# A two-block transformer layer on one core: overflow list in three spread steps, and differential attention with both distance products first and one softmax sum moved into the head's RMS norm

## The chip, the cores and the metric

The kernel runs on one core of a Trainium2 chip. The metric is the time of one execution on the device, in microseconds, as the median of several runs. TensorE is the matrix engine, VectorE, ScalarE and GpSimd (POOL) are the other engines, SyncE (SP) issues the weight transfers.

## The reference

Two blocks run one after the other on 512 tokens of 1024 features, all in float32. The first is a hybrid mixer followed by a mixture of experts (64 experts, 8 per token, 256 wide, and one shared expert). The second has two layers: latent attention with a feed-forward network, and then differential attention with a feed-forward network. The change touches the mixture of experts and the differential attention. Cut to those:

```python
def moe(h, w_router, router_bias, w1, w3, w2, ws1, ws3, ws2):
    ...
    counts = jnp.bincount(flat_e, length=N_EXPERTS)
    ...
    def expert_block(args):
        e, toks, gs = args
        xb = t[toks]
        return swiglu(xb, w1[e], w3[e], w2[e]) * gs[:, None]
    ...
    routed = jax.ops.segment_sum(out.reshape(rows, D), row_tok, num_segments=n_tok)

def _diff_mixer(x, w_in, lam_q1, lam_k1, lam_q2, lam_k2, g_sub, w_o, lambda_init):
    ...
    def block(args):                      # 128 queries, 8 heads, two maps m per head
        i, q_b = args
        q_pos = i * Q_BLOCK + jnp.arange(Q_BLOCK)
        dist = jnp.abs(q_pos[:, None] - k_pos[None, :]).astype(f32)
        logits = jnp.einsum('bqhmd,bkhmd->bmhqk', q_b, k, preferred_element_type=f32) * scale
        logits = logits - slopes[:, None, None] * dist
        logits = jnp.where(_chunk_mask(i * Q_BLOCK, s), logits, NEG_BIG)
        p = jax.nn.softmax(logits, axis=-1)
        a = p[:, 0] - lam * p[:, 1]
        o = jnp.einsum('bhqk,bkhe->bqhe', a.astype(v.dtype), v, preferred_element_type=f32)
        return o.astype(x.dtype)
    ...
    o = _rmsnorm(o, g_sub) * (1.0 - lambda_init)
    return o.reshape(b, s, DIFF_HEADS * DIFF_V) @ w_o
```

A head has 64 features per map and 128 for v; the mask lets a query see the keys up to the end of its chunk of 64.

## The kernel before

**Products.** Every float32 product is made of three passes over split operands (a high and a low part): `mm3` issues low x high, high x low and high x high into one PSUM bank (L228, L229, L230). The split itself is ScalarE's copy (L220, names wh, xet, ...) and VectorE's difference (L221, names wl, ...). `trs` transposes on TensorE (L233). PSUM has eight banks, handed out by `ps()`, named b in the trace.

**Weights.** `_Stream` loads weights on SyncE in the order of a job list (L112, name wraw), `raw` jobs ahead, and splits them. Its tiles come from a heap of 22 slots of 128x2048 (`slot`), from which xet, eo, ms and others are taken too; a slot is used again when its last reader is done, so a load can wait on any engine or on a transfer.

**Mixture of experts.** A list of ops is run in a loop; op by op an up product (both halves of an expert's first layer, L228 to L230 on xet) and a down product (L1412 on wraw and aet) follow, in a program order that is written out. Down results are scaled into eo (ScalarE L1414, VectorE L1416) and added to the accumulator in memory by a scattering transfer on POOL (L1217); rows are gathered on POOL (L1212). At op 40 `overflow()` (L1444) makes the list of pairs that did not fit an expert's capacity: counts (L1450, L1451), a chain of small VectorE operations for the capacities (L1454 to L1466), two matmuls (L1468, L1469), a second VectorE chain (L1471 to L1486, names tot, pl, ms), twelve matmuls (L1489) and copies to ll, li, nov (L1492 to L1497). All of it stands in one piece ahead of op 40's down product. The overflow blocks, which read ll, li and nov, come after the last op.

**Differential attention.** `pipeline` runs steps A, B, C, E, F, G, I for each head h and each block of 128 queries qt (nk = 128, 256, 384 or 512 keys), each with its own delay, and between them pieces of the projections of the next head pair as filling. A(h, qt) makes the logits of the two maps in two banks: a product of diag(h) with the distances (L2029), and three passes of q and k, which take rows 0 to 63 of the array for map 0 and rows 64 to 127 for map 1. B takes the maximum (L923, name nm) and the exponential with its sum (ScalarE L926). C combines the maps (L2043 to L2047): p0 is divided by its sum, r1 = -lam/s1, p0 = p1 * r1 + p0. E transposes and splits (pt), F multiplies by v. G squares the output with a sum (L2075), and at qt = 3 makes the norm of the head (`rsqrt`, L240 to L260) and scales into t2k (L2081). I transposes t2k (L233).

The indexer of the first block makes its scores by `mm3` as well, from 64-row operands: two heads that follow each other lie on rows 0 to 63 and 64 to 127 (names kit, qith, qitl).

Of the kernel before, what the change touches and what calls it, by code (L numbers as in the profile page):

```python
# [16 lines left out]
OP = mybir.AluOpType  # L17
# [6 lines left out]
NT = 4  # L24
# [6 lines left out]
NEG = -1e30  # L31
SLOTS = 22
FIX, PAIRS = 2, 16

CAPS = ((2, 128), (5, 192), (16, 128), (24, 96), (32, 80), (50, 64), (64, 48))
LR=9; LA=2; MOE_RAW=7
# [144 lines left out]
class _K:  # L181
# [735 lines left out]
        for _ in fill or ():  # L917
            pass

    def soft_exp(self, ps, nk, name, bufs):  # L920
        nc, V = self.nc, self.nc.vector
        nm = self.sm([128, 1], "nm", bufs=4)
        V.tensor_reduce(nm, ps[:, :nk], AX.X, OP.max, negate=True)  # L923
        p = self.sm([128, 512], name, bufs=bufs)
        sm = self.sm([128, 1], "sum", bufs=6)
        nc.scalar.activation(p[:, :nk], ps[:, :nk], AF.Exp, bias=nm, accum_out=sm)  # L926
        return p, sm

# [157 lines left out]
    def moe_block(self, hT, h2d, x1d):  # L1086
        nc, V, a, st = self.nc, self.nc.vector, self.a, self.st
        st.raw, st.ahead = MOE_RAW, 0
        late = slice(256, 512)
# [13 lines left out]
        acc = self.acc  # L1103
# [102 lines left out]
        def table_upto(n):  # L1206
            while nt[0] < min(n, NB):
                table_step(nt[0])
                nt[0] += 1
# [215 lines left out]
        def transpose_in(u):  # L1425
            if u < len(units):
                for b in range(first[u], first[u + 1]):
                    xT[b] = xpose(xg(b % 4))
# [15 lines left out]
        def overflow():  # L1444

            W = 96
            NB4 = 4
            psq = self.ps()
            for tt in range(NT):
                nc.tensor.matmul(psq[:NE, 0:2], Mp[:, tt], ones[:, 0:2], start=tt == 0, stop=tt == NT - 1)  # L1450
            nc.tensor.matmul(psq[:NE, 2:4], perm_b, evb, start=True, stop=True)  # L1451
            cap = self.sm([NE, 1], "cap", bufs=1)
            f2 = self.sm([NE, 1], "cap2", bufs=1)
            V.memset(cap, float(CAPS[0][1]))  # L1454
            for (e, c0), (_, c1) in zip(CAPS, CAPS[1:]):
                V.tensor_scalar(f2, pid[:NE], float(e), float(c1 - c0), OP.is_ge, OP.mult)
                V.tensor_tensor(out=cap, in0=cap, in1=f2, op=OP.add)
            base = self.sm([NE, NB4], "base", bufs=1)
            for b in range(NB4):
                V.tensor_scalar(base[:, b:b + 1], cap, 128.0 * b, None, OP.add)  # L1460
            cn = self.sm([NE, 4], "cn", bufs=1)
            V.tensor_copy(cn, psq[:NE, 0:4])
            fl = self.sm([NE, NB4], "fl", bufs=1)
            flb = self.sm([NE, NB4], "flb", BF16, bufs=1)
            V.tensor_tensor(out=fl, in0=cn[:, 0:1].to_broadcast([NE, NB4]), in1=base, op=OP.is_gt)
            V.tensor_copy(flb, fl)  # L1466
            psf = self.ps()
            nc.tensor.matmul(psf[:NE, 0:NB4], before[:NE, :NE], flb, start=True, stop=True)  # L1468
            nc.tensor.matmul(psf[:, NB4:2 * NB4], ones[:NE, :], flb, start=True, stop=True)  # L1469
            tot = self.sm([128, NB4 + 1], "tot", bufs=1)  # L1470
            V.memset(tot, 0.0)  # L1471
            for b in range(NB4):
                V.tensor_tensor(out=tot[:, b + 1:b + 2], in0=tot[:, b:b + 1], in1=psf[:, NB4 + b:NB4 + b + 1], op=OP.add)
            pl = self.sm([NE, NB4], "pl", bufs=1)
            V.tensor_tensor(out=pl, in0=tot[:NE, 0:NB4], in1=psf[:NE, 0:NB4], op=OP.add)
            V.scalar_tensor_tensor(pl, fl, -4096.0, pl, op0=OP.mult, op1=OP.add)
            V.tensor_scalar(pl, pl, 4096.0, None, OP.add)
            lst = self.ps()
            tmp = self.slot(F32, "ms")[:NE].bitcast(BF16)
            oh = tmp[:, 0:NB4 * W].rearrange("p (a b) -> p a b", b=W)  # L1480
            col = tmp[:, 1024:1024 + (NB4 + 2) * 128].rearrange("p (a b) -> p a b", b=128)
            V.tensor_copy(col[:, 0], cn[:, 2:3].to_broadcast([NE, 128]))
            V.tensor_copy(col[:, 1], pid[:NE].to_broadcast([NE, 128]))
            for b in range(NB4):
                V.tensor_scalar(oh[:, b], iota_b[:NE, :W], pl[:, b:b + 1], None, OP.is_equal)
                V.tensor_copy(col[:, 2 + b], base[:, b:b + 1].to_broadcast([NE, 128]))  # L1486
            for i in range(3):
                for b in range(NB4):
                    nc.tensor.matmul(lst[:, i * W:i * W + W], col[:, i if i < 2 else 2 + b], oh[:, b],  # L1489
                                     start=b == 0, stop=b == NB4 - 1)  # L1490
            ll = self.const.tile([128, 3, W + 1], F32, name="ll")
            V.memset(ll, 0.0)  # L1492
            V.tensor_copy(ll[:, :, 0:W], lst[:, 0:3 * W].rearrange("p (a b) -> p a b", b=W))
            li = self.const.tile([128, 1], I32, name="li")
            nov = self.const.tile([128, 1], I32, name="nov")
            V.tensor_copy(li, ll[:, 0, 0:1])
            V.tensor_copy(nov, tot[:, NB4:])  # L1497
            self.over = (ll, W), li, nov

        transpose_in(0)  # L1500
        for i, (op, u, m) in enumerate(ops):
            ranks, nb = units[u]
            if i == 2:
                for _ in shared_down():
                    table_upto(min(nt[0] + 1, 9))
            if i == 40:
                overflow()
            if i > len(ops) - 4:
                st.raw = 3
            if i == len(ops) - 8:  # L1510
# [22 lines left out]
            else:  # L1533
# [11 lines left out]
                for b, n in enumerate(nb):  # L1545
                    i = first[u] + b
# [6 lines left out]
        with self.tc.For_i(0, nreg) as _:  # L1553
# [27 lines left out]
            ps = self.ps()  # L1581
# [9 lines left out]
            c, cg = self.sm([128, 8, 3], "tc")[:, :1], self.sm([128, 8, 3], "tg")[:, :1]  # L1591
# [9 lines left out]
            ps = self.ps()  # L1601
# [362 lines left out]
    def diff_block(self, xT, xd, out, early):  # L1964
        nc, V, a, st = self.nc, self.nc.vector, self.a, self.st
# [16 lines left out]
        for i in range(2):  # L1982
            V.tensor_tensor(out=lp[:, i * 64:i * 64 + 64], in0=dc[:, 512 + i * 128:576 + i * 128],
                            in1=dc[:, 576 + i * 128:640 + i * 128], op=OP.mult)
        V.tensor_reduce(lam, lp.rearrange("p (a b) -> p a b", b=64), AX.X, OP.add)
        nc.scalar.activation(lam, lam, AF.Exp)
        nl = self.const.tile([128, 1], F32, name="nlam")
# [5 lines left out]
        def project(hp):  # L1993
# [23 lines left out]
                self.split(vd[:, tt * 256:tt * 256 + 256], vd[:, 1024 + tt * 256:1280 + tt * 256], ps[:, :256])  # L2017
                yield
            cur[hp] = (qd, kd, vd)
        lg, pr, pT, acc = {}, {}, {}, {}  # L2020

        def A(h, qt):
            qd, kd, _ = cur[h // 2]
            nk = (qt + 1) * 128
            o = (h % 2) * 512
            lg[h, qt] = []
            for m in range(2):
                p = self.ps()
                nc.tensor.matmul(p[:, :nk], diag(h), dr[:, 512 - nk:512], start=True, stop=False)  # L2029
                rw = slice(m * 64, m * 64 + 64)  # L2030
                self.mm3(p[:, :nk], (qd[rw, o + qt * 128:o + nk], qd[rw, 1024 + o + qt * 128:1024 + o + nk]),
                         (kd[rw, o:o + nk], kd[rw, 1024 + o:1024 + o + nk]), False, True)
                lg[h, qt].append(p)

        def B(h, qt):
            pr[h, qt] = [self.soft_exp(lg[h, qt][m], (qt + 1) * 128, f"p{m}", 3 - m) for m in range(2)]
            del lg[h, qt]

        def C(h, qt):
            (p0, s0), (p1, s1) = pr[h, qt]  # L2040
            nk = (qt + 1) * 128
            r0, r1 = self.sm([128, 1], "r0", bufs=4), self.sm([128, 1], "r1", bufs=4)
            V.reciprocal(r0, s0)  # L2043
            V.reciprocal(r1, s1)
            V.tensor_tensor(out=r1, in0=r1, in1=nl, op=OP.mult)
            V.tensor_scalar(p0[:, :nk], p0[:, :nk], r0, None, OP.mult)
            V.scalar_tensor_tensor(p0[:, :nk], p1[:, :nk], r1, p0[:, :nk], op0=OP.mult, op1=OP.add)  # L2047

        def E(h, qt):
# [22 lines left out]
        def G(h, qt):  # L2072
            po, ss = acc[h]
            j = self.t2k()
            nc.scalar.activation(j[:, :128], po[:, qt * 128:qt * 128 + 128], AF.Square, accum_out=ss[:, qt:qt + 1])  # L2075
            if qt == NT - 1:
                r = self.rsqrt(ss, NT, 1.0 / 128, 1e-6, "d_r")
                t = self.t2k()
                for i in range(NT):
                    q = slice(i * 128, i * 128 + 128)  # L2080
                    V.scalar_tensor_tensor(t[:, q], po[:, q], r[:, i:i + 1], gsub, op0=OP.mult, op1=OP.mult)  # L2081
                acc[h] = t
# [11 lines left out]
        def fill():  # L2094
            for hp in range(1, 4):
# [3 lines left out]
        st.raw, st.ahead = 2, 1  # L2099
        self.pipeline([(h, qt) for h in range(HEADS) for qt in range(NT)],  # L2100
                      [(A, 0), (B, 1), (C, 2), (E, 3), (F, 4), (G, 5), (I, 6)], fill(), 3,
                      lambda h, qt: h // 2 in cur)
        st.raw, st.ahead = 3, 1
# [52 lines left out]
```

## Time and profile before

| | |
|---|---|
| median of 3 runs | 2502.81 us (2502.02 to 2503.47) |
| profiled execution | 2503.96 us, its span 2502.2 us |
| mean granted clock of TensorE | 0.964 |
| TensorE busy | 2321.1 us, 93% of the span |
| VectorE busy | 1449.6 us, 58% |
| ScalarE busy | 941.1 us, 38% |
| bytes moved | 422.15 MB, mean 169 GB/s |

The profiled execution is one more run, not among the three; 1.76 us of it lie around the span. Rows of the trace give a start in us, a duration, the engine, the line, the operation with output and inputs, a count (several rows of one kind are drawn together), and in brackets the idle time ahead and what ended it. Matmuls overlap in a pipe, so the step from start to start tells what one costs, not its duration.

### The profile page before, as it was taken

How to read it: one execution, taken by the hardware profiler on the slowest of the kernel's cores; microseconds unless marked ns; L12 is line 12 of the kernel's file. 1: busy time of each engine (PE TensorE's matmuls, PEld its weight loads, DVE VectorE, ACT ScalarE, POOL GpSimd, SP SyncE). 2: the span in 40 equal slices, each digit the busy share in tenths (PEclk: the TensorE clock that was granted, in tenths of full speed). 3: DMA queues.
4: the chain of work that ended last, by engine and by line, in shares of the span. 5: the costliest groups of instructions: out<-in, count | busy, mean ns of one | idle time of the engine just before them, and what ended most of it. 6: DMA issues, size and time to landing. Idle time of an engine off the chain costs nothing.

```text
span 2502.2 us, 29499 instructions
## 1 busy us (share of the span) xinstructions
PE 2321.1 (93%) x11088; PEld 1805.0 (72%) x11088; DVE 1449.6 (58%) x2454; ACT 941.1 (38%) x1382; POOL 281.6 (11%) x184
## 2 busy tenths in 40 slices
PE   8877998799989999999699999999999998999998
PEld 4655767567667776676577788888888876888886
DVE  4599666666666765665576653333655657433235
ACT  1552443345545555555244222222234432322121
POOL 0652000122322222231000000000000000000000
PEclk9888999899999999999899999999999998999999
DMA  9442134599998999999402332232231121323310
GB/s 335 169 143 68 51 114 169 175 318 339 331 321 284 378 352 335 369 375 332 125 18 83 103 118 73 96 118 76 83 119 51 51 102 55 114 84 116 102 69 34
DMA packets 195009, 422.15 MB, mean 169 GB/s; under 512 B 21329, under 2 KB 99921, under 8 KB 186545
## 3 DMA queue, kind: packets, MB, share of 16 engines
q1 hardware_dynamic: 169984, 353.44, 39.8%
q0 software_dynamic: 12944, 39.20, 6.7%
q10 hardware_dynamic: 11938, 27.62, 3.0%
q8 instruction: 88, 1.44, 0.2%
q14 instruction: 55, 0.45, 0.1%
HBM read 390.78 MB, written 35.52 MB: 170 GB/s over the span
## 4 chain that ended last, share of the span: by engine, by line
PE 68%; DVE 16%; DMA 9%; ACT 4%; issue 2%; POOL 1%; ACTq 0%; SPq 0%; DVEq 0%; POOLq 0%
PE b L228 20%; PE b L229 19%; PE b L230 19%; PE b L1412 6%; DMA wraw<-in_w_dram 5%; DVE wl L221 4%; PE b L233 4%; DMA acc<-eo,isc 3%; ACT wh L220 2%; DVE work L754 1%; PE b L547 1%; DVE m L750 1%; DMA wraw<-in_w_ada_dram 1%; PE b L2029 1%; DVE y L1651 1%
## 5 line engine op out<-in xcount | busy, mean ns | idle before, releaser
L221 DVE TENSOR_TENSOR wl<-wraw,wh 128x2048 fp32r<-128x2048 f32 (+2 forms) x247 | 557.4, 2260 | 515.5 <-ACT wh L220 465.4
L220 ACT ACTIVATE wh<-wraw 128x2048 fp32r<-128x2048 f32 (+2 forms) x247 | 463.3, 1880 | 152.6 <-DVE wl L221 64.6
L228 PE MATMUL b<-xtl,wh 128*128 128x512 f32 (+1 forms) x928 | 343.5, 370 | 2.9 <-DVE xtl L221 2.9
L229 PE MATMUL b<-xth,wl 128*128 128x512 f32 (+1 forms) x928 | 341.6, 368 | 0.0
L230 PE MATMUL b<-xth,wh 128*128 128x512 f32 (+1 forms) x928 | 341.5, 368 | 0.0
L228 PE MATMUL b<-wl,xet 128*128 128x512 f32 x536 | 231.4, 432 | 15.3 <-DVE wl L221 14.9
L1412 PE MATMUL b<-wraw,aet 128*128 128x512 f32 x536 | 242.0, 595 | 0.8 <-ACT aet L1404 0.8
L230 PE MATMUL b<-wh,xet 128*128 128x512 f32 x536 | 214.2, 400 | 0.0
L229 PE MATMUL b<-wh,xet 128*128 128x512 f32 x536 | 213.1, 398 | 1.1 <-DVE xet L221 0.9
L228 PEld LDWEIGHTS b<-xtl,wh 128*128 128x128 f32 x928 | 176.1, 190 | 32.7 <-DVE xtl L221 3.6
L230 PEld LDWEIGHTS b<-xth,wh 128*128 128x128 f32 x928 | 175.8, 189 | 28.7
L229 PEld LDWEIGHTS b<-xth,wl 128*128 128x128 f32 x928 | 176.0, 190 | 28.0
L1412 PEld LDWEIGHTS b<-wraw,aet 128*128 128x128 f32 x536 | 98.9, 191 | 101.6 <-issue 97.0
L1217 POOL DMA_INDIRECT acc<-eo,isc x67 | 111.4, 1662 | 517.4 <-DMA acc<-eo,isc 126.9
L228 PE MATMUL b<-wl,ath 128*128 128x512 f32 x352 | 137.1, 390 | 0.0
L230 PE MATMUL b<-wh,ath 128*128 128x512 f32 x352 | 136.9, 389 | 0.0
L229 PE MATMUL b<-wh,atl 128*128 128x512 f32 x352 | 136.9, 389 | 0.0
L228 PEld LDWEIGHTS b<-wl,xet 128*128 128x128 f32 x536 | 103.2, 193 | 42.5 <-issue 20.3
L926 ACT ACTIVATE p<-b,nm 128x128 f32<-128x128 f32 (+3 forms) x128 | 67.0, 526 | 166.8 <-DVE nm L923 128.0
L229 PEld LDWEIGHTS b<-wh,xet 128*128 128x128 f32 x536 | 102.8, 192 | 28.6 <-issue 6.5
L230 PEld LDWEIGHTS b<-wh,xet 128*128 128x128 f32 x536 | 102.6, 191 | 23.1
L1933 ACT ACTIVATE t2k<-b 128x512 f32<-128x512 f32 x44 | 26.3, 599 | 185.9 <-PE b L230 185.9
(456 smaller groups left out, 4115.8 us busy)
## 6 DMA issues: line engine op xcount, KB each, us to landing
wraw<-in_w_dram SPq DMA_DIRECT2D x256, 512.0 KB, 11.2
wraw<-in_w_dram SPq DMA_DIRECT2D x64, 1024.0 KB, 9.7
wraw<-in_ffn_w_gu_dram SPq DMA_DIRECT2D x44, 1024.0 KB, 5.1
wraw<-in_w_ada_dram SPq DMA_DIRECT2D x24, 1024.0 KB, 10.4
wraw<-in_ffn_w_down_dram SPq DMA_DIRECT2D x20, 1024.0 KB, 4.9
wraw<-in_diff_w_in_dram SPq DMA_DIRECT2D x12, 1024.0 KB, 5.2
wraw<-in_w_in_dram SPq DMA_DIRECT2D x8, 1024.0 KB, 8.0
wraw<-in_w_in_dram SPq DMA_DIRECT2D x12, 512.0 KB, 5.0
```

The source lines that it names most:

```text
L220: nc.scalar.activation(H, x, AF.Copy)
L221: nc.vector.tensor_tensor(out=L, in0=x, in1=H.bitcast(F32), op=OP.subtract)
L228: mm(ps, s[0], m[1], start=start, stop=False)
L229: mm(ps, s[1], m[0], start=False, stop=False)
L230: mm(ps, s[0], m[0], start=False, stop=stop)
L233: self.nc.tensor.transpose(ps, x, self.ident[:x.shape[0], :x.shape[0]])
L547: nc.tensor.matmul(ps, cb[:, kc, :], w[:, kk, :], start=False, stop=kc == 7)
L750: V.max(m8[qt - 1], work(qt))
L926: nc.scalar.activation(p[:, :nk], ps[:, :nk], AF.Exp, bias=nm, accum_out=sm)
L1217: nc.gpsimd.indirect_dma_start(out=acc, out_offset=IndirectOffsetOnAxis(ap=idx, axis=0), in_=o, in_offset=None, compute_op=OP.add)
L1412: nc.tensor.matmul(ps, aT[:, f * 128:f * 128 + 128], w[:, f, c], start=f == 0, stop=f == 1)
L1933: nc.scalar.activation(sg, pss[j], AF.Silu)
```

## The change

The overflow list becomes a generator of three parts, at ops 40, 41 and 42 of the loop. The first ends after the capacity chain. The second (two matmuls, tot, pl and ms) is run one op later in the loop, the third (twelve matmuls, ll, li, nov) one more. A issues both distance products and then the passes of map 0 and of map 1. The exponentials of map 0 put their sums into one tile s0 of 128x4 per head; C no longer divides p0, and takes r1 = -lam * s0 / s1. The factor s0 that is left in the output is taken out in G: the sums of squares are multiplied twice by r0 = 1/s0 ahead of the norm, and the norm's factor once.

```diff
+OVER = 40
@@
-    def soft_exp(self, ps, nk, name, bufs):
+    def soft_exp(self, ps, nk, name, bufs, sm=None):
@@
-        sm = self.sm([128, 1], "sum", bufs=6)
+        if sm is None:
+            sm = self.sm([128, 1], "sum", bufs=6)
@@ overflow()
             V.tensor_copy(flb, fl)
+            yield
             psf = self.ps()
@@
-            lst = self.ps()
             tmp = self.slot(F32, "ms")[:NE].bitcast(BF16)
@@
+            yield
+            lst = self.ps()
             for i in range(3):
@@
             self.over = (ll, W), li, nov
+            yield
@@
-            if i == 40:
-                overflow()
+            if i == OVER:
+                late = overflow()
+            if i >= OVER:
+                next(late, None)
@@ def A(h, qt)
                 nc.tensor.matmul(p[:, :nk], diag(h), dr[:, 512 - nk:512], start=True, stop=False)
+                lg[h, qt].append(p)
+            for m, p in enumerate(lg[h, qt]):
                 rw = slice(m * 64, m * 64 + 64)
                 self.mm3(...)
-                lg[h, qt].append(p)
@@ def B(h, qt)
-            pr[h, qt] = [self.soft_exp(lg[h, qt][m], (qt + 1) * 128, f"p{m}", 3 - m) for m in range(2)]
+            if qt == 0:
+                s0[h] = self.sm([128, NT], "d_s0")
+            c = s0[h][:, qt:qt + 1]
+            pr[h, qt] = [self.soft_exp(lg[h, qt][m], (qt + 1) * 128, f"p{m}", 3 - m, None if m else c)
+                         for m in range(2)]
@@ def C(h, qt)
-            V.reciprocal(r0, s0)
             V.reciprocal(r1, s1)
-            V.tensor_tensor(out=r1, in0=r1, in1=nl, op=OP.mult)
-            V.tensor_scalar(p0[:, :nk], p0[:, :nk], r0, None, OP.mult)
+            V.scalar_tensor_tensor(r1, r1, nl, t0, op0=OP.mult, op1=OP.mult)
             V.scalar_tensor_tensor(p0[:, :nk], p1[:, :nk], r1, p0[:, :nk], op0=OP.mult, op1=OP.add)
@@ def G(h, qt)
             if qt == NT - 1:
+                r0 = self.sm([128, NT], "d_r0")
+                V.reciprocal(r0, s0.pop(h))
+                for _ in range(2):
+                    V.tensor_tensor(out=ss, in0=ss, in1=r0, op=OP.mult)
                 r = self.rsqrt(ss, NT, 1.0 / 128, 1e-6, "d_r")
+                V.tensor_tensor(out=r, in0=r, in1=r0, op=OP.mult)
```

Two places in TensorE's program show what moves. The first is the overflow list at op 40 (L1450 counts, L1468 and L1469 the two matmuls, L1489 the twelve, L1412 the down product, L1166 the next table step); before, from the last count on:

```order
L1450 MATMUL b<-ones,Mp 64x2
L1451 LDWEIGHTS perm_b
L1451 MATMUL b<-evb,perm_b 64x2
L1468 LDWEIGHTS before
L1468 MATMUL b<-flb,before 64x4
L1469 LDWEIGHTS ones
L1469 MATMUL b<-flb,ones 128x4
L1489 LDWEIGHTS ms
L1489 MATMUL b<-ms 128x96
```

Eleven more pairs on L1489 and then the eight L1412 follow (each is two records in the trace). After the change, from the same place (lines are one to four higher):

```order
L1452 MATMUL b<-ones,Mp 64x2
L1453 LDWEIGHTS perm_b
L1453 MATMUL b<-evb,perm_b 64x2
L1414 MATMUL b<-wraw,aet 128x512 x8
L1471 LDWEIGHTS before
L1471 MATMUL b<-flb,before 64x4
L1472 LDWEIGHTS ones
L1472 MATMUL b<-flb,ones 128x4
L1168 LDWEIGHTS P
L1168 MATMUL b<-idc,P 128x3
```

The down product now stands ahead of the two matmuls, and the twelve (now L1493) come some 40 rows later, between the up and the down product of op 41.

The second place is a group of step A, here the first with 512 keys (L2029 the distance, L228 to L230 the passes of q and k; the two numbers on b are the banks of map 0 and map 1). Before, up to the next transpose:

```order
L2029 MATMUL b_14783<-dr_14412 128x512
L228 MATMUL b_14783<-kd_14432,qd_14431 128x512
L229 MATMUL b_14783<-kd_14432,qd_14431 128x512
L230 MATMUL b_14783<-kd_14432,qd_14431 128x512
L2029 MATMUL b_14788<-dr_14412 128x512
L228 MATMUL b_14788<-kd_14432,qd_14431 128x512
L229 MATMUL b_14788<-kd_14432,qd_14431 128x512
L230 MATMUL b_14788<-kd_14432,qd_14431 128x512
L233 MATMUL b_14811<-ident_71,p0_14700 128x128
```

After:

```order
L2036 MATMUL b_14779<-dr_14412 128x512
L2036 MATMUL b_14781<-dr_14412 128x512
L229 MATMUL b_14779<-kd_14432,qd_14431 128x512
L230 MATMUL b_14779<-kd_14432,qd_14431 128x512
L231 MATMUL b_14779<-kd_14432,qd_14431 128x512
L229 MATMUL b_14781<-kd_14432,qd_14431 128x512
L230 MATMUL b_14781<-kd_14432,qd_14431 128x512
L231 MATMUL b_14781<-kd_14432,qd_14431 128x512
L234 MATMUL b_14803<-ident_71,p0_14701 128x128
```

The two distance products stand together, and the three passes of map 1 follow the three of map 0 directly.

## Rows read from the trace of the kernel before

**Rows 1.** The page, chain that ended last by engine, share of the span.
```profile
PE 68%; DVE 16%; DMA 9%; ACT 4%; issue 2%; POOL 1%; ACTq 0%; SPq 0%; DVEq 0%; POOLq 0%
```

**Rows 2.** Timeline of TensorE around the overflow list: start us, us, instruction, idle before.
```profile
725.37 3.60 PE L1412 MATMUL b<-wraw,aet 128*128 128x512 f32 x8
...
741.57 0.21 PE L1468 MATMUL b<-flb,before 64*64 64x4 bf16 x1 [5.08 <-DVE tot L1471]
...
743.58 1.74 PE L1489 MATMUL b<-ms 64*128 64x96 bf16 x12 [1.68 <-DVE ms L1485]
745.24 8.52 PE L1412 MATMUL b<-wraw,aet 128*128 128x512 f32 x16
```

**Rows 3.** Busy us by stretch: PE, PEld, DVE, ACT, POOL, clock, DMA share, GB/s.
```profile
740.00:760.00 20.00, 16.61 (x68) 10.21 (x69) 9.88 (x39) 3.56 (x4) 3.01 (x2) 0.83 0.51 155
...
2010.00:2020.00 10.00, 10.00 (x67) 8.03 (x65) 5.01 (x18) 3.99 (x13) 0.00 (x0) 1.00 0.00 1
...
2030.00:2040.00 10.00, 7.23 (x22) 5.35 (x23) 8.84 (x30) 2.76 (x11) 0.00 (x0) 0.66 0.40 155
```

**Rows 4.** Timeline of VectorE in the overflow list.
```profile
738.55 0.14 DVE L1456 TENSOR_SCALAR cap<-pid 64x1 f32<-64x1 f32 x1
...
741.93 0.16 DVE L1473 TENSOR_TENSOR tot<-tot,b 128x1 f32<-128x1 f32 x1 [0.41 <-PE b L1469]
...
744.31 0.21 DVE L1486 CAST ms<-base 64x128 bf16<-64x128 f32 x1
```

**Rows 5.** Waits of SyncE's queue, 600 to 900: us in total, times, longest.
```profile
SPq L112 <- DMA acc<-eo,isc: 39.4, 4, 23.1
```

**Rows 6.** Timeline of POOL: the second scatter after the overflow list.
```profile
758.46 1.44 POOL L1217 DMA_INDIRECT acc<-eo,isc  x1 [5.55 <-DMA acc<-eo,isc]
```

**Rows 7.** Timeline of TensorE: one group of step A with 512 keys.
```profile
2017.13 0.39 PE L2029 MATMUL b<-dr 128*128 128x512 f32 x1
2017.45 0.50 PE L228 MATMUL b<-kd,qd 64*128 64x512 f32 x1
2017.78 0.39 PE L229 MATMUL b<-kd,qd 64*128 64x512 f32 x1
2018.02 0.39 PE L230 MATMUL b<-kd,qd 64*128 64x512 f32 x1
2018.34 0.49 PE L2029 MATMUL b<-dr 128*128 128x512 f32 x1
2018.76 0.49 PE L228 MATMUL b<-kd,qd 64*128 64x512 f32 x1
...
2019.65 0.33 PE L233 MATMUL b<-ident,p 128*128 128x128 f32 x1
```

**Rows 8.** Timeline of TensorE: scores of the indexer, two heads at a time.
```profile
121.33 0.50 PE L228 MATMUL b<-kit,qith 64*128 64x512 f32 x2
121.66 0.40 PE L229 MATMUL b<-kit,qitl 64*128 64x512 f32 x2
121.90 0.40 PE L230 MATMUL b<-kit,qith 64*128 64x512 f32 x2
...
122.92 0.50 PE L228 MATMUL b<-wl,hth 128*128 128x512 f32 x1
```

**Rows 9.** Groups of VectorE, 1851 to 2096, by form: busy us, mean ns, idle before.
```profile
L2045 DVE TENSOR_TENSOR r<-r,nlam 128x1 f32<-128x1 f32 x32 | 5.1, 160 | 1.1
...
L2046 DVE TENSOR_SCALAR p<-p,r 128x512 f32<-128x512 f32 x8 | 3.8, 480 | 0.0
```

**Rows 10.** Timeline of VectorE: start of the unbroken stretch after 1907.
```profile
1907.88 2.29 DVE L221 TENSOR_TENSOR wl<-wraw,wh 128x2048 fp32r<-128x2048 f32 x1 [1.38 <-ACT wh L220]
```

**Rows 11.** Timeline of TensorE: two of its waits in the differential attention.
```profile
1915.89 0.66 PE L233 MATMUL b<-ident,t2k 128*128 128x128 f32 x4 [0.19 <-DVE t2k L2081]
...
2032.77 0.79 PE L228 MATMUL b<-wl,mixoh 128*128 128x512 f32 x1 [3.85 <-ACT p L926]
```

**Rows 12.** Waits of TensorE, 1851 to 2096: us in total, times, longest.
```profile
PE b L233 <- DVE t2k L2081: 4.6, 4, 2.9
```

More of the change, by code (lines that the diff above doesn't have):

```diff
@@ L2019, in project @@
             cur[hp] = (qd, kd, vd)
-        lg, pr, pT, acc = {}, {}, {}, {}
+        lg, pr, pT, acc, s0 = {}, {}, {}, {}, {}
         def A(h, qt):
@@ L2032, in A @@
                          (kd[rw, o:o + nk], kd[rw, 1024 + o:1024 + o + nk]), False, True)
-                lg[h, qt].append(p)
         def B(h, qt):
-            pr[h, qt] = [self.soft_exp(lg[h, qt][m], (qt + 1) * 128, f"p{m}", 3 - m) for m in range(2)]
+            if qt == 0:
[3 more added lines that the diff above has]
+                         for m in range(2)]
             del lg[h, qt]
         def C(h, qt):
-            (p0, s0), (p1, s1) = pr[h, qt]
+            (p0, t0), (p1, s1) = pr[h, qt]
             nk = (qt + 1) * 128
-            r0, r1 = self.sm([128, 1], "r0", bufs=4), self.sm([128, 1], "r1", bufs=4)
-            V.reciprocal(r0, s0)
+            r1 = self.sm([128, 1], "r1", bufs=4)
             V.reciprocal(r1, s1)
-            V.tensor_tensor(out=r1, in0=r1, in1=nl, op=OP.mult)
-            V.tensor_scalar(p0[:, :nk], p0[:, :nk], r0, None, OP.mult)
+            V.scalar_tensor_tensor(r1, r1, nl, t0, op0=OP.mult, op1=OP.mult)
             V.scalar_tensor_tensor(p0[:, :nk], p1[:, :nk], r1, p0[:, :nk], op0=OP.mult, op1=OP.add)
```

## The prediction

> **What bounds the kernel now.** I read the chain of waits first, then three stretches: the overflow list in the MoE, the distance and logit products of the differential attention, and an earlier stage of the same kernel that already holds the pattern which the change makes. TensorE carries 68% of the chain [rows 1], so a gain has to be an idle gap of TensorE that closes, or TensorE time that goes while its neighbours keep up.
>
> In the overflow list both exist. TensorE idles 5.08 us before L1468, which waits for the capacity chain on VectorE, and 1.68 us before L1489, which waits for ms; 12 small products then take 1.74 us, and the sixteen L1412 records after them need 8.52 us [rows 2]. In that 20 us window TensorE is busy 16.61 us, its granted clock is 0.83, and the DMA share is 0.51 [rows 3]. In the differential attention (1851 to 2096) TensorE has no idle in most windows, as at 2010 [rows 3], with VectorE busy half the time; what counts there is how long each group on L2029 and L228 to L230 is.
>
> **Overflow list, part by part.** Part 1 stays where it was, but TensorE now goes on to the sixteen L1412 records. The capacity chain runs on VectorE from 738.55 until L1468 starts at 741.57 [rows 2, 4]. L1412 would start where the gap began, 741.57 - 5.08 = 736.5. Ten microseconds earlier eight such records took 3.60 with the clock at its full 2.4 GHz [rows 2], some 0.43 each, so sixteen last 6.9 us; the 8.52 of now comes from the half clock, 1.2 GHz, after the two gaps, which the window's 0.83 holds. It ends near 743.4, after the chain, so the two matmuls of part 2 wait for nothing. Before, L1412 ended at 745.24 + 8.52 = 753.8 [rows 2]. That is 753.8 - 743.4 = 10.4 us earlier. Back go the two matmuls of part 2, in line with other short ones (0.35), and the 12 of part 3 at full clock (12 x 0.1 = 1.2, at most the 1.74 of now). Part 3's inputs come from VectorE work that lasts from 741.9 to 744.5 before [rows 4] and now stands behind the same down product: some 3 us, and a whole up product of TensorE lies between, so I take its wait at zero. The sum is **10.4 - 1.6 = 8.8 us**.
>
> Behind part 3's wait stands op 41's down product, and nobody else waits; ll, li and nov are read only by the overflow blocks after the last op. The order on SyncE and POOL doesn't change. Which slot a weight load takes does, because ms is made later: the load that now waits 23.1 us for a scatter [rows 5] takes a slot last read by matmuls before that down product. I estimate SyncE idle for 10 us instead of 23. The transfers come back sooner than TensorE gains, so they don't eat the 8.8. But the slot of the scattered tile goes to a wh, so that ScalarE's split now stands behind the second scatter, which was issued at 758.46 [rows 6] and will be issued some 8 us earlier. My estimate is 0 to 4 us on ScalarE, of which about 1 reaches TensorE, since the split is made some microseconds ahead of its use. I put the MoE at **-8** (8.8 - 0.8), between -5 (a full 4 us wait) and -10.
>
> **Logit products.** A group with 512 keys is, before the change: distance, three passes of map 0, distance, three passes of map 1. Its starts run from 2017.13 to 2019.65, 2.52 us, eight matmuls [rows 7]. Two passes of one kind follow each other at 2018.02 - 2017.78 = 0.24; the steps between a 128-row and a 64-row matmul are 0.32, 0.33, 0.32 and 0.42. The change puts both distance products first, so one of the two round trips goes, and sets map 0's passes (rows 0 to 63) next to map 1's (rows 64 to 127). What two such sets cost side by side is shown by the indexer's scores on L228 to L230, where two heads lie on the same halves of the rows and come in the same program order, three passes of one and then three of the other: the records start in pairs ("x2"), 121.33, 121.66, 121.90, so twelve matmuls of 512 columns last 122.92 - 121.33 = 1.59 us instead of 12 x 0.23 = 2.8 [rows 8]. A pair costs what one costs.
>
> So the new group is 0.23 (distance) + 0.32 + three pairs (0.33 + 0.24 + 0.33) = 1.45, and saves 1.07: three passes of 0.23 (0.69) and one round trip (0.38). For 384, 256 and 128 keys I scale the passes with the columns and keep the 0.38: 0.90, 0.73, 0.55. One head has all four, 3.25 us; eight heads give **26 us** of TensorE time. The bounds: without pairing 0.1 to 0.38 per group is left (3 to 12 us); below nothing it can't go, since the same eight matmuls run with fewer switches.
>
> **VectorE.** Per group it loses one reciprocal, one product of 128x1 (0.16) and one scaling of p (0.48 at 512) [rows 9]. In eight heads G gains a reciprocal and three products of 128x4, about 0.2 each with the wait on the one before: +0.8. Where VectorE already ends last, part of the 26 is lost. From 1907.88 [rows 10] to 1916 it runs without a break, from the weight split over two maxima to the norm of a head and the t2k scaling, and TensorE waits 0.19 for t2k [rows 11]; the two groups in that stretch (256 and 128 keys, 1.3 us) are lost there, and the chain is 0.8 - 0.4 longer: 1.7 us. The same pattern comes once more, 60 us on (1.7). At 2032.77 TensorE waits 3.85 for ScalarE's exp behind four transfers and a split; part of a group ahead of that is lost (0.6) [rows 11]. The waits for t2k come to 4.6 us in four places [rows 12], most of it in the last head; there I lose 1.2. In the other heads the timeline shows VectorE idle ahead of G's work, more than the few tenths that a head gains. Sum: 26 - 3.4 - 0.6 - 1.2 = 20.8, and for a clock drop after one of the new gaps I take off 0.3: **-20.5**.
>
> Both parts: -28.5. The profiled execution took 2503.96 us (span 2502.2, and 1.76 around it) and would take 2475.5; it lies 1.15 above the median of the runs, 2502.81, so the median becomes **2474**.
>
> **The rivals.**
> 1. *Pairs only where they touch.* TensorE keeps program order, so that only the last pass of map 0 runs beside the first of map 1. Each group then saves one pass and the round trip: 0.62, 0.56, 0.50, 0.45, some 17 us, less 5 lost: -12, and with the MoE -20: 2483. For: nothing but the order of the program. The Trainium skill, "TensorE: Matmul & The Clock Gate" (Part 3, The mechanism), says that matmuls start and end in strict program order, which would make this the outcome; the scores disagree, with same-line records starting in pairs though the program lists them three passes apart [rows 8]. Chance 8%.
> 2. *No pairing.* The scores' pairs could come from something that this group lacks (here the accumulation starts with a full-height matmul). Then 3 to 12 us of TensorE less some 3 of waits, with the MoE: -8 to -17, about 2490. Chance 7%.
> 3. *VectorE or the weight stream takes more.* If a third of the heads are held by VectorE instead of two and the last, or the wh slot keeps TensorE waiting 4 us, 7 to 9 us are lost: 2482. VectorE's 5.01 of 10 us [rows 3] is room on the average, not at the pinches. Chance 8%.
> 4. *Slower: waits that drop the clock.* With shorter groups VectorE could end last in all eight heads, the whole 20.5 be lost to gaps, and each gap be followed by some 5 us at 1.2 GHz instead of 2.4, as after 2032.77, where the window's clock is 0.66 [rows 3]: 8 x 2.5 = 20 more. Total -8 + 20 = +12: 2515. It decides from four such drops on, with the gain all lost. Against it: the two pinches of now have gaps of 0.2 only [rows 11]. Chance 3%, with another 2% for ending within 0.2%.
> 5. *The overflow list brings nothing*, because transfers hold TensorE anyway: -20, 2482. Against it: both gaps are ended by VectorE, not by a transfer [rows 2]. Chance 2%.
>
> **The numbers.** The forecast, 2474 with its own bounds 2465 to 2482 (MoE -5 to -10, the pinches 3 to 8 us, pairs as the scores' [rows 8] or a little better), has 70%. The range that holds it 8 times in 10 reaches to rivals 1, 3 and 5 and the near part of 2: 2465 to 2488. About 0.2% (5 us) is what a measurement can tell from no change. Faster: the forecast, 1, 2, 3 and 5 together, 0.95; the same 0.02; slower 0.03.
>
> **What would show it.** Right: the 5.08 and 1.68 gaps gone, no L1414 record at half clock, SyncE's longest wait for a scatter under 15 us; logit passes L229 to L231 on kd as x2 rows with starts 0.24 apart and a 512 group of 1.4 to 1.5 us; the stage from 1851 to 2096 some 20 us shorter, with two new gaps of 1 to 2 us before a transpose of t2k. Wrong: single rows on kd (rival 1 or 2), a wait of wh for a scatter with TensorE idle behind it, a granted clock of half in many windows of that stage.

## The result, and the profile after

The changed kernel takes 2478.28 us (median of 4 runs, 2476.24 to 2479.69) against 2502.41 of the kernel before (4 runs): ratio 0.9899, 95% interval 0.9885 to 0.9914, so 24.1 us less where 28.5 were forecast. The profiled execution of after took 2478.60 us, its span is 2476.8, the granted clock 0.963.

The chain of the page is still TensorE's; the share of DMA in it fell from 9% [rows 1] to 6%.

```profile
PE 69%; DVE 17%; DMA 6%; ACT 5%; issue 2%; POOL 1%; ACTq 0%; SPq 0%; DVEq 0%; POOLq 0%
```

**Overflow list.** Timeline of TensorE, after; it answers to [rows 2]:

```profile
733.74 7.13 PE L1414 MATMUL b<-wraw,aet 128*128 128x512 f32 x16
740.81 0.19 PE L1471 MATMUL b<-flb,before 64*64 64x4 bf16 x1
740.93 0.17 PE L1472 MATMUL b<-flb,ones 64*128 64x4 bf16 x1
...
748.07 0.68 PE L1493 MATMUL b<-ms 64*128 64x96 bf16 x12
...
766.80 0.77 PE L229 MATMUL b<-wl,xet 128*128 128x512 f32 x1 [3.87 <-DVE wl L222]
```

Both gaps are gone: the down product runs at full clock (7.13 us with its last record's end, before 8.52), and neither the two small matmuls nor the twelve on ms (L1493) wait for anything. But 26 us behind the two small ones there is a new gap of 3.87 us. ScalarE's timeline shows whose it is:

```profile
755.70 0.38 ACT L1406 ACTIVATE aet<-b 128x256 f32<-128x256 f32 x1 [2.59 <-PE b L234]
762.42 1.91 ACT L221 ACTIVATE wh<-wraw 128x2048 fp32r<-128x2048 f32 x1 [6.33 <-DMA acc<-eo,isc]
```

A split stood 6.33 us behind the second scatter. The stretches of TensorE show the price: the window that had 16.61 us busy [rows 3] is full now, and the next one, full before, has 16.13 with a clock of 0.83. The second window before, and then both after:

```profile
760.00:780.00 20.00, 20.00 (x98) 14.08 (x97) 14.19 (x17) 12.07 (x14) 6.14 (x4) 1.00 0.90 256
```

```profile
740.00:760.00 20.00, 20.00 (x111) 14.51 (x110) 13.83 (x35) 7.11 (x9) 5.39 (x3) 1.00 1.00 336
760.00:780.00 20.00, 16.13 (x62) 10.55 (x61) 11.78 (x13) 10.88 (x12) 6.57 (x4) 0.83 0.90 260
```

Both programs have the same 11088 matmul records in nearly the same order, so they can be lined up one by one. Across the overflow list (records 2940 to 3110) TensorE gains 9.05 us; in the 150 records behind it loses 6.96 again. SyncE's longest wait for a scatter, 600 to 900, fell from 23.1 [rows 5] to 8.0 us:

```profile
SPq L113 <- DMA acc<-eo,isc: 15.3, 3, 8.0
```

**Differential attention.** A group with 512 keys, timeline of TensorE, after; it answers to [rows 7]:

```profile
1996.67 0.63 PE L2036 MATMUL b<-dr 128*128 128x512 f32 x2
1997.23 0.51 PE L229 MATMUL b<-kd,qd 64*128 64x512 f32 x2
1997.57 0.40 PE L230 MATMUL b<-kd,qd 64*128 64x512 f32 x2
1997.81 0.39 PE L231 MATMUL b<-kd,qd 64*128 64x512 f32 x2
1998.13 0.33 PE L234 MATMUL b<-ident,p 128*128 128x128 f32 x1
```

The passes come in pairs, and the group lasts 1998.13 - 1996.67 = 1.46 us instead of 2.52. The groups with 384, 256 and 128 keys last 1.17, 0.88 and 0.75 (before 2.07, 1.62 and 1.37), and all 32 groups together 34.3 us instead of 60.9. The whole stage, from its first product to the next network (records 7920 to 9600), before and then after; the first number behind the length is TensorE's busy time, the clock is third from the end:

```profile
1842.16:2155.32 313.16, 295.11 (x1683) 244.13 (x1681) 191.59 (x488) 112.84 (x288) 0.00 (x0) 0.96 0.21 71
```

```profile
1834.58:2129.99 295.41, 270.59 (x1682) 231.54 (x1681) 188.96 (x458) 111.20 (x290) 0.00 (x0) 0.95 0.23 75
```

The stage is 17.75 us shorter. TensorE is busy 24.5 us less, but idles 24.8 instead of 18.05. The granted clock summed over the stage gives 27.3 us at the half clock (1.2 GHz) before and 30.7 after, so, if TensorE was busy in these stretches, 1.7 us of the busy time after is the slower clock, and the work itself shrank by 26.2, close to the 26.6 of the groups. The waits of TensorE, 1840 to 2080, answer to [rows 12]:

```profile
PE b L234 <- DVE t2k L2097: 9.7, 4, 3.5
PE b L229 <- ACT p L928: 4.5, 1, 4.5
```

Of the 25.4 us between the two profiled executions 5.2 have no part of the change in them: 3.1 us lie in the first 240 records and 2.1 around 1445 us, ahead of the first feed-forward network, where the kernel before had run longer at the half clock; the change touches neither place.

### The profile page after: what moved, and what is told of

Its sections match the earlier page's. It is cut to its first block, busy times and chain, and to the rows that moved or that the text cites. A ratio compares the mean times of both kernels' runs of the same rounds, so it can differ in the third digit from the quotient of the medians.

```text
span 2476.8 us, 29476 instructions
## 1 busy us (share of the span) xinstructions
PE 2293.9 (93%) x11088; PEld 1791.6 (72%) x11088; DVE 1445.9 (58%) x2422; ACT 938.8 (38%) x1382; POOL 280.3 (11%) x184
## 4 chain that ended last, share of the span: by engine, by line
PE 69%; DVE 17%; DMA 6%; ACT 5%; issue 2%; POOL 1%; ACTq 0%; SPq 0%; DVEq 0%; POOLq 0%
PE b L229 20%; PE b L230 19%; PE b L231 19%; PE b L1414 7%; DMA acc<-eo,isc 4%; PE b L234 4%; DVE wl L222 4%; ACT wh L221 2%; DVE work L755 1%; PE b L548 1%; DVE m L751 1%; DMA wraw<-in_w_ada_dram 1%; DVE y L1658 1%; DVE nm L924 1%; DVE y L1657 1%
## 5 line engine op out<-in xcount | busy, mean ns | idle before, releaser
L230 PE MATMUL b<-xth,wl 128*128 128x512 f32 (+1 forms) x928 | 341.2, 368 | 0.0
L230 PE MATMUL b<-wh,xet 128*128 128x512 f32 x536 | 214.3, 400 | 0.9 <-DVE xet L222 0.8
L230 PEld LDWEIGHTS b<-xth,wl 128*128 128x128 f32 x928 | 175.5, 189 | 28.2
L230 PE MATMUL b<-wh,atl 128*128 128x512 f32 x352 | 136.9, 389 | 0.0
L230 PEld LDWEIGHTS b<-wh,xet 128*128 128x128 f32 x536 | 104.0, 194 | 28.0 <-issue 6.2
```

The source lines that it names most:

```text
L230: mm(ps, s[1], m[0], start=False, stop=False)
```

## The experiments

All runs are compared with the kernel before on the same chip; runs 1 to 4, 5 to 8 and 9 to 12 were on three different ones. A kernel's runs spread over 3 to 16 us there, so the times decide only what is far apart. The rest is decided by the gaps in the profiles, above all the two pinches: the two places in the middle of the differential attention where TensorE waits for t2k, whose gaps repeat to some hundredths from profile to profile.

**1. The overflow list alone.** Kernel before with this edit:

```diff
-            if i == 40:
-                overflow()
+            if i == OVER:
+                late = overflow()
+            if i >= OVER:
+                next(late, None)
```

and the three `yield`s of the change.

> Kernel before with the overflow list in three steps alone; attention as before. Theory 1 (the two gaps close, and the split that now takes the slot of the scattered tile waits for the second scatter and gives most of it back): TensorE 9 us earlier after the overflow list, 6 to 7 us lost again behind the scatter, in all 1 to 4 us faster than before. Theory 2 (the forecast: the wait hardly reaches TensorE): 7 to 9 us faster.

Measured: 2497.27 us against 2501.82, ratio 0.9973 (0.9961 to 0.9984). TensorE gained the same 9.05 us across the list and lost 2.2 behind the scatter, where ScalarE's split waited 3.8 us; the profiled run was the fastest of the ten, 2493.0. Timeline of TensorE:

```profile
763.51 0.47 PE L229 MATMUL b<-wl,xet 128*128 128x512 f32 x1 [1.35 <-DVE wl L222]
```

The mechanism is theory 1's, the time lies between the two: how much is lost again differs with the split's wait, which was 6.33 us in the changed kernel's profile and 3.82 here.

**2. Step A alone.** Kernel before with the two lines of A moved:

```diff
+                lg[h, qt].append(p)
+            for m, p in enumerate(lg[h, qt]):
                 rw = slice(m * 64, m * 64 + 64)
...
-                lg[h, qt].append(p)
```

> Kernel before with the new order in step A alone; softmax sums and overflow list as before. Theory 1 (pairs of passes give the whole gain, and the sum put into the norm lengthens VectorE's chain where VectorE ends last): groups of 1.45 us at 512 keys, 18 to 22 us faster than before, so at least as much as the differential attention of the changed kernel gained (17.8). Theory 2 (the shorter C is needed so that VectorE keeps up): 10 to 15 us faster.

Measured: 2481.61 us against 2501.82, ratio 0.9914 (0.9891 to 0.9937). The stage is 19.3 us shorter than before, 1.6 more than with the whole change. The two pinches, timeline of TensorE:

```profile
1905.54 0.66 PE L233 MATMUL b<-ident,t2k 128*128 128x128 f32 x4 [1.55 <-DVE t2k L2082]
...
1961.17 1.11 PE L233 MATMUL b<-ident,t2k 128*128 128x128 f32 x4 [1.55 <-DVE t2k L2082]
```

So the pairs give the gain, and the relief in C isn't needed for it: theory 1.

**3. The sum in the norm alone.** Kernel before with the edits of B, C and G.

> Kernel before with the first map's sum put into the norm alone; order of step A and overflow list as before. Theory 1 (TensorE bounds the stage outside the pinches, the pinches get 0.4 us longer): 0 to 2 us slower than before, nothing that the runs can tell. Theory 2 (VectorE's work in C counts): 2 to 5 us faster.

Measured: 2506.5 us against 2501.82, ratio 1.0016 (1.0003 to 1.0029): 4.7 us slower, more than theory 1 allowed. Both pinches grew from 0.19 [rows 11] and 0.20 to 1.02:

```profile
1913.78 0.66 PE L233 MATMUL b<-ident,t2k 128*128 128x128 f32 x4 [1.02 <-DVE t2k L2090]
...
1973.94 0.80 PE L233 MATMUL b<-ident,t2k 128*128 128x128 f32 x4 [1.02 <-DVE t2k L2090]
```

In this profile the stage is 6.1 us longer: 2.3 more idle, and 37.5 instead of 27.3 us at the half clock, which costs half the difference, 5.1, less 1.3 of shorter work. Of these 10.2 us, 3.4 lie behind the second pinch, the rest in and behind the last head. Theory 1 had the sign and the pinches, but in this profile the clock that fell cost more than the gaps.

**4. The three steps at op 41.** Changed kernel with another number:

```diff
-OVER = 40
+OVER = 41
```

> Changed kernel with the three steps at ops 41, 42 and 43, so that the slot of the scattered tile goes to a weight load on SyncE and no longer to a split on ScalarE. Theory 1 (the split's wait for the scatter costs 6 to 7 us): ScalarE waits for no scatter near 760, and the time is 4 to 7 us below the changed kernel, 2471 to 2475. Theory 2 (TensorE has run ahead of the weight transfers and loses it in any arrangement): same time as the changed kernel, 2478.

Measured: 2477.72 us against 2501.82, ratio 0.9893 (0.9872 to 0.9913), the changed kernel's within the interval, as theory 2 said. ScalarE waits no more near 760, but at 783.15 for the scatter of the next tile, whose slot also goes to a split:

```profile
783.15 1.91 ACT L221 ACTIVATE wh<-wraw 128x2048 fp32r<-128x2048 f32 x1 [3.85 <-DMA acc<-eo,isc]
```

TensorE stood 1.38 us behind it and lost 1.9 there. The wait was moved, not removed. Theory 2 has the time, theory 1 the place: the loss goes where the split's wait goes. That the smaller loss doesn't show in the time is in part the clock: the profiled run, the slowest of the four (2482.62), had 37.5 us at the half clock in the differential attention, the changed kernel's 30.7.

**5. Overflow list and step A, without the sum.** The first two edits together.

> Changed kernel without the move of the first map's sum into the norm (overflow list in three steps and the new order in step A). Theory 1 (the sum in the norm only lengthens the two pinches and the tail): the two gaps before the transposes of t2k are 1.55 us instead of 2.37, and the time is 1 to 4 us below the changed kernel, 2475 to 2477. Theory 2 (the relief in C is worth it): 2 to 5 us above it.

Measured: 2476.99 us against 2502.12, ratio 0.9891 (0.9868 to 0.9915). The gaps are 1.53, without the overflow list 1.55. Theory 1 holds in the gap; the 1.3 us below the changed kernel's first median can't be told by time. Why the sum costs 0.83 a pinch and not 0.4 is seen in VectorE's timeline of the stretch. This run first:

```profile
1896.51 0.15 DVE L2050 RECIPROCAL r<-sum 128x1 f32<-128x1 f32 x1
...
1896.83 0.41 DVE L2053 TENSOR_SCALAR p<-p,r 128x384 f32<-128x384 f32 x1
1897.28 0.62 DVE L2054 SCALAR_TENSOR_TENSOR p<-p,r,p 128x384 f32<-128x384 f32 x1
1897.81 0.42 DVE L222 TENSOR_TENSOR pt<-b,pt 128x256 fp32r<-128x256 f32 x1
1898.15 0.16 DVE L241 TENSOR_SCALAR rs_t<-d_ss 128x4 f32<-128x4 f32 x1
```

and the changed kernel:

```profile
1897.16 0.15 DVE L2056 RECIPROCAL r<-sum 128x1 f32<-128x1 f32 x1
1897.35 0.22 DVE L2057 SCALAR_TENSOR_TENSOR r<-r,nlam,d_s 128x1 f32<-128x1 f32 x1
1897.60 0.62 DVE L2058 SCALAR_TENSOR_TENSOR p<-p,r,p 128x384 f32<-128x384 f32 x1
1898.43 0.42 DVE L222 TENSOR_TENSOR pt<-b,pt 128x256 fp32r<-128x256 f32 x1 [0.21 <-ACT pt L221]
1898.78 0.17 DVE L2089 RECIPROCAL d_r<-d_s 128x4 f32<-128x4 f32 x1
1899.05 0.36 DVE L2091 TENSOR_TENSOR d_ss<-d_ss,d_r 128x4 f32<-128x4 f32 x2
1899.44 0.17 DVE L241 TENSOR_SCALAR rs_t<-d_ss 128x4 f32<-128x4 f32 x1
...
1901.23 0.16 DVE L2093 TENSOR_TENSOR d_r<-d_r,d_r 128x4 f32<-128x4 f32 x1
```

C is shorter: its last operation starts 0.44 us behind its first, in run 5 0.77. But VectorE then waits 0.21 for ScalarE's half of the split of pt, which comes behind two exponentials, and the split starts 1.27 us behind C's first operation, in run 5 1.30: C's relief is gone at once. The additions in G stay whole: 1899.44 - 1898.78 = 0.66 ahead of the norm and 0.2 behind it.

**6. Step I one step later.** Changed kernel with

```diff
-                      [(A, 0), (B, 1), (C, 2), (E, 3), (F, 4), (G, 5), (I, 6)], fill(), 3,
+                      [(A, 0), (B, 1), (C, 2), (E, 3), (F, 4), (G, 5), (I, 7)], fill(), 3,
```

> Changed kernel with step I (the transposes of t2k) one step later in the pipeline. Theory 1 (TensorE loses at the pinches because it reaches the transposes before VectorE has made t2k, and the half clock comes from these gaps): both gaps of 2.37 us and the half clock behind them go, nothing is lost elsewhere, 4 to 8 us below the changed kernel, 2470 to 2474. Theory 2 (VectorE bounds the stage there, so that the next wait takes the gap over): the gaps come back before the transposes of p, same time.

Measured: 2479.44 us against 2502.12, ratio 0.9908 (0.9886 to 0.9931). Theory 1 fell (first pinch, timeline of TensorE):

```profile
1903.56 0.50 PE L229 MATMUL b<-xtl,wh 128*128 128x512 f32 x1 [2.36 <-DVE t2k L2097]
```

Both gaps keep their size to 0.02 us and stand before a filling product now, so theory 2 was right that another wait takes them over, but not which. That product writes b and doesn't read t2k: what it can wait for is its PSUM bank, the head's output, which VectorE's t2k reads last. So t2k has to end early, whoever reads it.

**7. Overflow list and step A, with step I later.**

> The kernel of the run with overflow list and step A alone, with step I one step later. Theory 1: with the pinches gone the sum in the norm matters in the tail only, so this is within 1 us of the run with step I later, 2470 to 2474. Theory 2 (C's relief counts once the pinches are gone): 2 to 4 us above that run.

Measured: 2472.42 us (4 runs, 2467.21 to 2473.66) against 2502.12, ratio 0.9873 (0.9849 to 0.9897). That is 7.0 below run 6, which neither theory has. The gaps are 1.53, as in run 5, so step I isn't what made it faster. The stage had 27.3 us at the half clock in this profile, in run 5 it had 34.1; run 10 is the same kernel again.

**8. As run 6, with the reload on SyncE.** The four transfers of y in the out projection's first half move from ScalarE's queue:

```diff
-            X.append(self.reload(xd))
+            X.append(self.reload(xd, nc.sync))
```

with `reload` issuing on the engine it is given.

> Changed kernel with step I one step later and the four reloads of the residual (y from xd) issued by SyncE instead of ScalarE. Theory 1 (the 4.48 us gap before the out projection's first half is ScalarE's: 2.45 us of issuing ahead of the split): that gap is 2 to 2.5 us, and the time is 2 to 4 us below the run with step I later. Theory 2 (the gap is the weight's arrival): no change of the gap.

Measured: 2479.48 us against 2502.12, ratio 0.9905 (0.9884 to 0.9927). Timeline of TensorE:

```profile
2011.63 0.50 PE L229 MATMUL b<-wl,mixoh 128*128 128x512 f32 x1 [1.88 <-ACT p L928]
...
2016.72 0.55 PE L234 MATMUL b<-ident,p 128*128 128x128 f32 x3 [1.28 <-DVE t2k L2097]
```

The gap fell from 4.49 in run 6 to 1.88, by 2.6 where theory 1 had 2.45, and a part came back as a wait for t2k, 1.28. The time didn't follow: the stage had 37.5 us at the half clock in this profile, in run 6 30.7. A gain of 1 us isn't to be shown with these runs.

**9. The slot to a load.** The kernel of run 7, with one more weight load ahead for six ops, which shifts the heap by a tile so that no split takes the scattered tiles' slots there:

```diff
+            if 42 <= i <= 48:
+                st.raw = 10 if i < 48 else LR
```

> The kernel of the run with overflow list, step A and step I later, with one more weight load ahead (10 instead of 9) during ops 42 to 47, so that the slot of the scattered tile goes to a load on SyncE. Theory 1 (the split's wait for the scatter makes the loss near 766): no wait of ScalarE's split for a scatter between 750 and 775, no gap of TensorE there, TensorE keeps the 9 us to within 1, and the time is 2 to 4 us below the run with overflow list, step A and step I later. Theory 2 (weight transfers are late there in any arrangement): the gap stays, now behind a load.

Measured: 2472.88 us (4 runs, 2471.29 to 2474.39) against 2501.44, ratio 0.9883 (0.9861 to 0.9906). No split of ScalarE waits for a scatter between 735 and 800. The loss window of the changed kernel is full:

```profile
760.00:780.00 20.00, 20.00 (x98) 14.06 (x97) 14.41 (x17) 12.08 (x14) 6.08 (x5) 1.00 0.95 302
```

TensorE keeps its 9.05 us to 0.02. SyncE's queue waits for scatters now (waits of SyncE, 735 to 800):

```profile
SPq L113 <- DMA acc<-eo,isc: 21.2, 4, 8.8
```

and that costs TensorE nothing here. Theory 1, but the time is further below run 10 than its 2 to 4 us; run 10 shows why.

**10. Run 7's kernel again,** beside run 9.

> The same kernel as the run with overflow list, step A and step I one step later (no sum in the norm), once more beside the others. If its 2472.4 came from step I: 4 to 6 us below the changed kernel again. If it came from chance in the half clock and in the scatter: 1 to 3 us below it.

Measured: 2479.54 us (5 runs, 2477.70 to 2481.90) against 2501.44, ratio 0.9910 (0.9891 to 0.9930): 1.9 us below the changed kernel beside it, 7.1 above its own median of before. So 2472.42 was not step I's. On one chip run 9 is 6.7 us below run 10, and their programs differ only in the one more load ahead that moves the slot. The profiled executions, 6.6 apart, show that the loss at the slot's place is a part of it. There run 10 loses 4.3 us and run 9 nothing. Another 5.9 lie near 950, where ScalarE's split stands behind a later scatter, as it did in the kernel before. The kernel before, then run 10 and run 9 with ScalarE's row and TensorE's:

```profile
950.70 1.91 ACT L220 ACTIVATE wh<-wraw 128x2048 fp32r<-128x2048 f32 x1 [8.63 <-DMA acc<-eo,isc]
```

```profile
947.23 1.91 ACT L221 ACTIVATE wh<-wraw 128x2048 fp32r<-128x2048 f32 x1 [9.89 <-DMA acc<-eo,isc]
951.61 0.77 PE L229 MATMUL b<-wl,xet 128*128 128x512 f32 x1 [5.20 <-DVE wl L222]
```

```profile
940.48 1.91 ACT L221 ACTIVATE wh<-wraw 128x2048 fp32r<-128x2048 f32 x1 [5.22 <-DMA acc<-eo,isc]
944.86 0.47 PE L229 MATMUL b<-wl,xet 128*128 128x512 f32 x1 [0.54 <-DVE wl L222]
```

Run 7, the same kernel as run 10 on another chip, had the short wait too, 5.20 with a gap of 0.51, and its profiled execution was 5.9 us below run 10's. So the short wait near 950 can come without the slot, and that the slot brought it in run 9 is not shown. In the differential attention run 9 was 2.9 us longer than run 10, with 37.5 us at the half clock and not 30.7. The slot is shown to be worth the 4.3 us at its own place.

**11. The changed kernel again.**

> The changed kernel once more, beside the others: 2476 to 2480. TensorE's gap behind the scatter is ScalarE's wait less 2.45 us again, whatever the wait is this time; the two gaps before the transposes of t2k are 2.37 us again.

Measured: 2481.44 us (6 runs, 2473.95 to 2483.68) against 2501.44, ratio 0.9914 (0.9895 to 0.9934). Its median is 1.4 us above the expected range. ScalarE's wait and TensorE's gap, one fence from each engine's timeline:

```profile
763.91 1.91 ACT L221 ACTIVATE wh<-wraw 128x2048 fp32r<-128x2048 f32 x1 [6.03 <-DMA acc<-eo,isc]
```

```profile
768.29 0.77 PE L229 MATMUL b<-wl,xet 128*128 128x512 f32 x1 [3.56 <-DVE wl L222]
```

6.03 - 3.56 = 2.47. The first profile gave 6.33 - 3.87 = 2.46, run 4's other tile 3.85 - 1.38 = 2.47. The pinches were 2.36 each.

**12. The passes in turn.** Changed kernel with the order of the six passes changed:

```diff
-            for m, p in enumerate(lg[h, qt]):
-                rw = slice(m * 64, m * 64 + 64)
-                self.mm3(...)
+            for x, y in ((0, 1024), (1024, 0), (0, 0)):
+                for m, p in enumerate(lg[h, qt]):
+                    rw = slice(m * 64, m * 64 + 64)
+                    nc.tensor.matmul(p[:, :nk], qd[rw, x + o + qt * 128:x + o + nk],
+                                     kd[rw, y + o:y + o + nk], start=False, stop=not (x or y))
```

> Changed kernel with the passes of the two maps issued in turn (first of map 0, first of map 1, second of map 0, and so on). Theory 1 (TensorE pairs matmuls of different row groups whatever their order within a few instructions): groups as in the changed kernel, 1.45 us at 512 keys. Theory 2 (strict order, so that neighbours pair best): groups shorter by 0.1 to 0.3 us.

Measured: one run, 2483.8 us. The group (all six passes are on one line now):

```profile
1886.84 0.63 PE L2036 MATMUL b<-dr 128*128 128x512 f32 x2
1887.40 0.97 PE L2041 MATMUL b<-kd,qd 64*128 64x512 f32 x6
1888.30 0.33 PE L234 MATMUL b<-ident,p 128*128 128x128 f32 x1
```

1888.30 - 1886.84 = 1.46, as with three and three: theory 1.

## Why the prediction was right, and where it was off

The time lay in the range, 4 us above the forecast. By its own steps:

- **"10.4 - 1.6 = 8.8 us"** for the overflow list: right. Lined up record by record, the nine later profiles with the steps at op 40 gained 9.05 us each, too.
- **"0 to 4 us on ScalarE, of which about 1 reaches TensorE"**: this step failed. The wait was 3.0 to 6.3 us in the nine profiles with this slot, TensorE's gap is that less 2.46, and half of the time at 1.2 GHz behind the larger gaps comes on top: 1.35 to 6.96 us given back, the most in the first profile (gap and clock account for it to within 0.9 us). I had found the slot and the queue, but took the landing of the second scatter from an issue 8 us earlier. It was issued only 6.1 us earlier (752.39 for 758.46) and took 9.9 us to land (762.27), where in the kernel before it had taken 4.8, so it landed only 1.0 us earlier. The DMA share of that window is 1.00, before 0.51 [rows 3]; that the load on the transfers made the scatter slower is likely, but not shown. Run 9 is the test of the slot: with it given to a load, the loss is gone.
- **"eight heads give 26 us"** of the logit products: right, 26.6 by the groups. The pairs are what they were in the scores [rows 8]. Rival 1 is out by the paired rows of the changed kernel and by run 12, whose order would have made the group shorter if only neighbours paired, and left it at 1.46 us. The Trainium skill, "TensorE: Matmul & The Clock Gate" (Part 3, The mechanism), has matmuls start and end in strict program order; the traces disagree, 1.46 us in both orders.
- **"the chain is 0.8 - 0.4 longer"** at the pinches: the 0.8 was right, but hardly any of the 0.4 was to be had, since C's relief ended in a wait for ScalarE (run 5). With 1.53 of gap from the shorter groups and 0.83 from the sum, each pinch is 2.37 instead of 0.19. TensorE's idle time in the stage rose by 6.8 us, where the forecast gave 5.2.
- **"for a clock drop after one of the new gaps I take off 0.3"**: 1.7 in the first profile, 3.4 in run 11. Of the two gaps of 2.37 us one was followed by the half clock, the other not:

```profile
1900.00:1910.00 10.00, 7.63 (x33) 5.86 (x31) 6.81 (x25) 2.96 (x12) 0.00 (x0) 0.83 0.00 1
...
1950.00:1960.00 10.00, 7.63 (x46) 6.28 (x45) 9.11 (x29) 2.81 (x11) 0.00 (x0) 1.00 0.22 86
```

So the stage comes to 26.2 - 6.8 - 1.7 = 17.7 us, forecast 20.5, and the MoE to 9.05 - 6.96 + 0.7 (the drift up to its end) = 2.8, forecast 8. Their sum is 20.5, where 28.5 were forecast and the medians show 24.1. In the profiled pair the rest is the 5.2 us in places that the change doesn't touch, and on the chip of run 11 the changed kernel was 20.0 us below the kernel before. So a part of how near the first time came to 2474 is luck; how the 3.6 us of the medians divide stays open.

The rivals: slower by clock drops (4) had the right mechanism for run 3, which was slower by 4.7 us, but the 26 us of the pairs are far above it. Rival 3 is the nearest to what happened, and its 2482 fits run 11's 2481.44 better than the forecast does. Of its two mishaps one came, the split's wait, at up to 7 us; the other came in another form: VectorE held TensorE in the forecast's places, two heads and the last, but at 2.2 us per pinch and not 1.7.

The version that the experiments point to, run 9, leaves the sum out of the norm and gives the slot to a load: 2472.88 us, ratio 0.9883, 8.6 us below the changed kernel on the same chip; a part of that is the shorter wait near 950, which isn't shown to come from the slot.

## What to carry to other kernels

Two sets of 64-row matmuls that stand next to each other on the two halves of the rows cost here what one set costs (six passes of 512 columns 0.90 us, three of them before 0.89 [rows 7]), so it pays to bring them together, and a stage of the same kernel that has them already gives the price beforehand. Where tiles come from one heap, a moved allocation changes who waits for whom: look up which engine takes the slot of every tile that a slow transfer reads, and see that it is a load ahead of need, not a split on whose result the next product waits. The place near 950, where the kernel before already had such a split, shows that it is worth looking for more than one. Work taken off VectorE was worth almost nothing at the pinch, because its next input wasn't there yet (0.21 us of waiting in run 5's comparison); work added where it ended last was paid in full (0.83 us a pinch).

## What was not expected of the hardware

TensorE's gap behind the split was the split's wait less 2.46 us in every profile with that wait, to 0.02, and near 950 the wait less 4.68 in all fourteen, to 0.01. The clock wasn't so regular: a gap of 1.02 us (run 3, at 1973.94) was followed by the half clock and one of 2.37 (1958.91, after) was not, and two kernels with the same gaps in this stage to 0.3 us, runs 7 and 9, had 27.3 and 37.5 us at the half clock, a difference of 5 us in time. The same kernel in two comparisons on two chips, runs 7 and 10, came out 7 us apart with no run of the one inside the spread of the other; between the two profiled executions the difference arises near 950, behind one split.
